# Transposes in an encoder trunk: squares of 32 on VectorE and a DRAM write and read in place of TensorE transposes

## The chip, the cores and the metric

The kernel runs on one core of a Trainium2 chip. The metric is the device time of one launch in microseconds (us). The engines are named as the profile names them: PE is the matrix engine (TensorE), PEld its weight loads, DVE is VectorE, ACT is ScalarE, POOL is GpSimd, and SP is the engine whose queue issues the DMAs (SPq).

## The reference

The reference is an encoder trunk of two layers over 256 tokens of width 2048, in float32. In each layer the normalised input `h` goes through one combined projection, which gives queries, keys and values of three attention branches, a gate path for each branch, and three merge gates:

```python
for l in range(DEPTH):
    h = rmsnorm(x, pre_norm_g[l])
    proj = jnp.einsum('bsd,dn->bsn', h, w_in[l])
    (qa, ka, va, qb, kb, vb, qc, kc, vc, za, zb, zc, gates) = jnp.split(proj, split_points, axis=-1)
    ya = neighbourhood_attention(heads(qa, 8), heads(ka, 8), heads(va, 8), rpb[l])
    qb_h = axial_rope(rmsnorm(heads(qb, 8), q_norm_g[l]))
    kb_h = axial_rope(rmsnorm(heads(kb, 2), k_norm_g[l]))
    yb = gqa_attention(qb_h, kb_h, heads(vb, 2))
    yc = dilated_mixture(heads(qc, 12), heads(kc, 12), heads(vc, 12))
    ga, gb, gc = jnp.split(sigmoid(gates + b_gate[l]), 3, axis=-1)
    merged = (ga * ((ya * silu(za)) @ w_branch_a[l]) + gb * ((yb * silu(zb)) @ w_branch_b[l])
              + gc * ((yc * silu(zc)) @ w_branch_c[l]))
    x = x + rmsnorm(merged @ w_out[l], post_norm_g[l])
```

## The kernel before

The 256 tokens are two tiles T of 128. All weights are streamed from DRAM in chunks of 256 rows by 512 columns (512 KB): `emit_raw` (L155 to L166) loads a chunk on SP's queue, `emit_hi` (L171, ACT) rounds it to a high part `wh`, and `emit_lo` (L176, DVE) takes the rest `wl`. `run_half` (L192) multiplies a chunk for one token tile. Each product is made of three one-pass matmuls (`mm3`, L143 to L148: high by high, high by low, low by high), so one chunk is 12 matmuls of 512 columns. There are 704 chunks: 8 for each block of 512 output columns of the combined projection and of the output projection, 4 or 2 for each block of the branch products.

The order of the work is written out by hand. The loop at the end of `trunk` (L737 to L753) goes through the chunks; `ahead` (L179) issues loads up to 6 chunks ahead, high parts up to 3 ahead and low parts up to 2 ahead. After each chunk `slot` (L100) puts in side work: two steps of the block evacuations in `evq`, one step of each generator in `active`, and one new job, from the queue `light` if it has one that is due, else from `heavy`. A `yield` ends a job's step for that slot. Each engine and SP's queue work in this program order.

Most tiles (`U`, L59) come from one pool of 47 buffers of 4 KB a partition.

A projection arrives with tokens on the partitions; what is contracted next must have columns on the partitions. So there are transposes on PE, [128,128] by an identity, four side by side in a bank of PSUM `tp`:

- `tr_job` (L280, its matmuls L284) for queries, keys and gate paths: one job for each token tile, started in the slot after the evacuation (or one later). ACT and DVE then split `tp` into high and low (L130, L132), or ACT copies it (L289).
- `head_job` (L360), 16 heads a layer of branches A and B: scores, softmax and norm in two slots; two slots on, four transposes of the probabilities (L380) and one split; two slots on, the product with the values `o` and `gate`. Heads start two slots apart (the 2 in `heavy`).
- `job_c` (L407), 4 merged heads a layer: the same with four transposes for each tile (L140 by `four_T`), heads four slots apart.
- `mt_job` in `merge` (L568): four transposes for each tile of the merged branches (L140), split into `MT[nb]`, the stationary operand of the output projection. `merge(3)` is followed at once by `out_block(0)`, whose chunk 6 (of 0 to 7) is the first to use `MT[3]`.
- `ht_psum` (L247): the next layer's input, also by `four_T`.

All DMAs are issued by SP in program order: chunks, the gate biases (`bg`, L553), the post-norm gains (L605), `x` (L73, L600).

Of the kernel before, what the change touches and what calls it, by code (L numbers as in the profile page):

```python
# [20 lines left out]
P = 128  # L21
GRID_W = 64
EPS = 1e-6
# [8 lines left out]
class Blk:  # L32
    """One 512-column block of a projection: K chunks of 256 rows, both token tiles."""
# [14 lines left out]
def trunk(ctx, tc, x, xT, wpack, wbr_a, wbr_b, wbr_c, wout, pre_g, qk_g, bgate, post_g, abias,  # L48
# [32 lines left out]
    # the engines wake while the first loads are under way  # L81
# [8 lines left out]
    evq, light, heavy, active = deque(), deque(), deque(), []  # L90
    flow = dict(cool=0, hold=True, slot=0, split=9)

    def later(g, wait=0):
        """a filler for a following slot, once what it needs is under way"""
        light.append((flow["slot"] + wait, g))
# [26 lines left out]
    def rsqrt(v, n):  # L122
        """1/sqrt of a small positive f32 tile"""
        y = small.tile([P, n], F32, name="rs_y")
        nc.gpsimd.tensor_tensor(out=y, in0=v, in1=mhalf[:, :n], op=ALU.pow)
        return y

    def split(src, h, lo, scale=1.0):
        """src * scale -> h + lo, both exactly representable for the one-pass products."""
# [6 lines left out]
    def four_T(src):  # L136
        """Four [128,128] transposes side by side in one bank."""
        tp = aux.tile([P, 4, P], F32, name="tp", bufs=2)
        for j in range(4):
            nc.tensor.transpose(tp[:, j, :], src(j), ident)  # L140
        return tp

    def mm3(out_, lhs, rhs, first, last):  # L143
        """out_ += lhs.T @ rhs for (high, low) pairs: one-pass products"""
# [60 lines left out]
    prev = {}  # L205

    def layer(l):
# [6 lines left out]
        # -- the layer's input: hT = (x * gain) transposed, 1/rms kept apart --  # L214
# [24 lines left out]
        def ht_x(nb, js):  # L239
            """from the host's transposed layout of x"""  # L240
# [6 lines left out]
        def ht_psum(nb, T):  # L247
            """from the previous layer's output: residual, transposes"""
# [30 lines left out]
        # -- evacuations, per token tile --  # L279
        def tr_job(dst, tok, T, n=4):  # L280
            """token-major [tok, n x 128] -> dst[column, block, tokens of T]; a pair is split"""
            tp = aux.tile([P, 4, P], F32, name="tp", bufs=2)
            for j in range(n):
                nc.tensor.transpose(tp[:, j, :], tok[:, T, j * P:(j + 1) * P], ident)  # L284
            c = slice(T * P, (T + 1) * P)
            if isinstance(dst, tuple):
                split(tp[:, 0:n], dst[0][:, 0:n, c], dst[1][:, 0:n, c])
            else:
                nc.scalar.copy(dst[:, 0:n, c], tp[:, 0:n])  # L289
            yield  # L290

        def evac_qk(store, key, which, two):
            tok = {}

            def f(T, ps):
# [4 lines left out]
                later(tr_job(store[key], tok[0], T))  # L300
# [16 lines left out]
        def evac_z(key):  # L317
            tok = {}

            def f(T, ps):  # L320
# [6 lines left out]
                later(tr_job(SZ[key], tok[0], T), 1)  # L327
# [3 lines left out]
        # -- attention --  # L331
        def softmax(sc, p, n, w, f=None):
            """n x w logits a row: exp(f * (s - max)), and the sums"""
# [11 lines left out]
        def norm(p, sm, n, rsh):  # L345
            """rows divided by their sums, times the gate's factor of the token"""
# [13 lines left out]
        def head_job(zb, hh, q, k, v, bias=None, f=None):  # L360
            """one head over all 256 keys, both token tiles: q, k give (high, low) of [d, tokens],
            v those of [keys of a tile, d]"""
# [14 lines left out]
            tp = aux.tile([P, 2, 256], F32, name="tp", bufs=2)  # L377
            for T in range(2):
                for kk in range(2):
                    nc.tensor.transpose(tp[:, kk, T * P:(T + 1) * P], p[:, T, kk * P:(kk + 1) * P], ident)  # L380
            pp = U("pp", [2, 2, 256], FR)
            ph, pl = pp[:, 0], pp[:, 1]
            split(tp, ph, pl)
# [23 lines left out]
        def job_c(hh, dist):  # L407
            """one merged head: the three groups' keys under one softmax"""
# [24 lines left out]
            px = U("px", [2, 256])  # L433
            for T in range(2):
                c = slice(T * P, (T + 1) * P)
                tp = four_T(lambda j: ps_[T][:, 0, j * P:(j + 1) * P])
                split(tp[:, 0:2], ph[:, :, c], pl[:, :, c])
                nc.scalar.copy(px[:, :, c], tp[:, 2:4])
                yield
# [10 lines left out]
        # -- branch A: two units of four heads --  # L450
# [17 lines left out]
        # -- branch B --  # L468
# [10 lines left out]
        def rope(dst, ps, T, n, which):  # L479
            """dst = rotation of ps (n heads), the norm's gain in the tables; in two steps"""  # L480
# [15 lines left out]
        def head_norm(ps, T, n):  # L496
            """1/rms of each head (of the normalised input's projection)"""
# [8 lines left out]
        def evac_qb(u):  # L506
            tok = {}

            def f(T, ps):
# [7 lines left out]
                later(tr_job(QT["b", u], tok[0], T), 1)  # L517
                if T == 1:
                    for hh in range(4):
                        heavy.append((2, job_b(u, hh)))  # L520
            return f

        def evac_kvb(T, ps):
# [14 lines left out]
            later(tr_job(KT["b"], tok, T, n=2), 1)  # L538
# [7 lines left out]
        # -- gates and branch products --  # L546
        def merge(nb):
# [20 lines left out]
            def mt_job(T):  # L568
                if nb not in MT:
                    MT[nb] = pair("mT", [4, 256])  # L570
                h, lo = MT[nb]
                c = slice(T * P, (T + 1) * P)
                tp = four_T(lambda j: G[0][:, T, j * P:(j + 1) * P])
                split(tp, h[:, :, c], lo[:, :, c], scale=0.5)
                yield

            def evac_p(i):
                def f(T, ps):
# [3 lines left out]
                    if i == 1:  # L582
                        later(mt_job(T))
# [268 lines left out]
```

## Time and profile before

| what | value |
|---|---|
| median of 3 runs | 2075.62 us (2074.99 to 2075.86) |
| span of the profiled execution, first to last instruction | 2073.5 us |
| median less that span (what lies around it) | 2.1 us |
| PE busy | 2061.9 us (99%), 9634 matmuls |
| DVE busy | 1163.2 us (56%) |
| ACT busy | 951.4 us (46%) |
| moved by DMA | 397.81 MB, mean 192 GB/s |
| TensorE clock granted | 9 in every slice (90% of full speed or more), mean 0.999 |

The profile is of one execution. Its own time outside the profiler is not given apart from its span, so the span and the 2.1 us that the median lies above it stand for it. Busy shares are of the span. A row such as `L284 PE MATMUL tp<-ident,tok` names the line, the engine, the operation, and the tile written from the tiles read. PE's durations overlap, because matmuls are pipelined; what one costs is read from the distance between starts.

### The profile page before, as it was taken

How to read it: one execution, taken by the hardware profiler on the slowest of the kernel's cores; microseconds unless marked ns; L12 is line 12 of the kernel's file. 1: busy time of each engine (PE TensorE's matmuls, PEld its weight loads, DVE VectorE, ACT ScalarE, POOL GpSimd, SP SyncE). 2: the span in 40 equal slices, each digit the busy share in tenths (PEclk: the TensorE clock that was granted, in tenths of full speed). 3: DMA queues.
4: the chain of work that ended last, by engine and by line, in shares of the span. 5: the costliest groups of instructions: out<-in, count | busy, mean ns of one | idle time of the engine just before them, and what ended most of it. 6: DMA issues, size and time to landing. Idle time of an engine off the chain costs nothing.

```text
span 2073.5 us, 24944 instructions
## 1 busy us (share of the span) xinstructions
PE 2061.9 (99%) x9634; PEld 1716.2 (83%) x9634; DVE 1163.2 (56%) x1445; ACT 951.4 (46%) x1370; POOL 23.2 (1%) x31
## 2 busy tenths in 40 slices
PE   9999999999999999999999999999999999999998
PEld 7888888888888888888888888888888888888886
DVE  6444466565776554645554445565657764646454
ACT  6443354444554434443564444454445543443332
POOL 0000000000000000000000000000000000000000
PEclk9999999999999999999999999999999999999999
DMA  9555455645546655667565554555454466656662
GB/s 373 190 173 187 153 173 179 213 156 185 168 163 208 203 198 188 203 228 259 174 228 171 188 183 142 182 176 200 164 187 163 168 213 200 197 191 208 228 241 71
DMA packets 115270, 397.81 MB, mean 192 GB/s; under 512 B 12752, under 2 KB 12880, under 8 KB 115152
## 3 DMA queue, kind: packets, MB, share of 16 engines
q1 hardware_dynamic: 115152, 396.23, 56.5%
q8 instruction: 75, 1.23, 0.2%
q14 instruction: 43, 0.35, 0.1%
HBM read 391.99 MB, written 4.19 MB: 191 GB/s over the span
## 4 chain that ended last, share of the span: by engine, by line
PE 99%; DMA 0%; ACT 0%; DVE 0%; SPq 0%; issue 0%; DVEq 0%; POOLq 0%; ACTq 0%
PE acc L148 31%; PE acc L146 31%; PE acc L147 31%; PE tp L284 1%; PE tp L140 1%; PE tp L380 1%; PE o L148 0%; PE sc L148 0%; PE o L147 0%; PE sc L147 0%; PE o L146 0%; PE sc L146 0%; DMA raw<-in_wpack_dram 0%; PE o L446 0%; PE sc L418 0%; DVE x L597 0%
## 5 line engine op out<-in xcount | busy, mean ns | idle before, releaser
L176 DVE TENSOR_TENSOR wl<-raw,wh 128x1024 fp32r<-128x1024 f32 (+1 forms) x706 | 831.7, 1217 | 172.1 <-ACT wh L171 169.3
L146 PE MATMUL acc<-wh,hTh 128*128 128x512 f32 x2240 | 886.3, 396 | 0.6 <-ACT wh L171 0.6
L147 PE MATMUL acc<-wl,hTh 128*128 128x512 f32 x2240 | 873.8, 390 | 0.8 <-DVE wl L176 0.8
L148 PE MATMUL acc<-wh,hTl 128*128 128x512 f32 x2240 | 873.8, 390 | 0.0
L171 ACT CAST wh<-raw 128x1024 fp32r<-128x1024 f32 (+1 forms) x706 | 699.3, 1043 | 40.0 <-DVE wl L176 12.9
L148 PEld LDWEIGHTS acc<-wh,hTl 128*128 128x128 f32 x2240 | 420.6, 188 | 89.0
L147 PEld LDWEIGHTS acc<-wl,hTh 128*128 128x128 f32 x2240 | 421.5, 188 | 84.9 <-DVE wl L176 2.6
L146 PEld LDWEIGHTS acc<-wh,hTh 128*128 128x128 f32 x2240 | 421.2, 188 | 83.3 <-ACT wh L171 1.6
L564 ACT ACTIVATE g<-g 128x512 f32<-128x512 f32 x48 | 30.4, 633 | 232.8 <-DVE g L563 232.8
L563 DVE SCALAR_TENSOR_TENSOR g<-acc,rsx,bg 128x512 f32<-128x512 f32 x48 | 35.9, 747 | 173.6 <-PE acc L148 173.6
L146 PE MATMUL acc<-wh,yTh 128*128 128x512 f32 x320 | 124.5, 389 | 0.0
L147 PE MATMUL acc<-wl,yTh 128*128 128x512 f32 x320 | 124.5, 389 | 0.0
L148 PE MATMUL acc<-wh,yTl 128*128 128x512 f32 x320 | 124.5, 389 | 0.0
L146 PE MATMUL acc<-wh,mTh 128*128 128x512 f32 x256 | 100.4, 392 | 0.0
L148 PE MATMUL acc<-wh,mTl 128*128 128x512 f32 x256 | 99.7, 390 | 0.0
L147 PE MATMUL acc<-wl,mTh 128*128 128x512 f32 x256 | 99.7, 389 | 0.0
L299 ACT ACTIVATE tok<-acc,rsx 128x512 f32<-128x512 f32 x40 | 27.6, 689 | 124.9 <-PE acc L148 124.9
L340 ACT ACTIVATE sp<-sp,nm 128x256 f32<-128x256 f32 (+1 forms) x48 | 27.6, 577 | 109.4 <-DVE nm L335 109.4
L579 DVE SCALAR_TENSOR_TENSOR g<-g,acc 128x512 f32<-128x512 f32 x48 | 32.8, 683 | 78.6 <-PE acc L148 78.6
L147 PEld LDWEIGHTS acc<-wl,yTh 128*128 128x128 f32 x320 | 60.1, 188 | 12.5
L146 PEld LDWEIGHTS acc<-wh,yTh 128*128 128x128 f32 x320 | 60.1, 188 | 12.5
L130 ACT ACTIVATE mTh<-tp 128x512 fp32r<-128x512 f32 x16 | 9.6, 598 | 132.4 <-PE tp L140 132.4
(116 smaller groups left out, 1172.2 us busy)
## 6 DMA issues: line engine op xcount, KB each, us to landing
raw<-in_wpack_dram SPq DMA_DIRECT2D x558, 512.0 KB, 3.5
raw<-in_wo_dram SPq DMA_DIRECT2D x64, 512.0 KB, 5.2
raw<-in_wa_dram SPq DMA_DIRECT2D x32, 512.0 KB, 3.3
raw<-in_wb_dram SPq DMA_DIRECT2D x32, 512.0 KB, 3.7
raw<-in_wc_dram SPq DMA_DIRECT2D x16, 512.0 KB, 3.8
bg<-in_bgate_dram SPq DMA_DIRECT2D x24, 256.0 KB, 3.8
x<-in_x_dram SPq DMA_DIRECT2D x8, 512.0 KB, 7.9
abias<-in_abias_dram SPq DMA_DIRECT2D x8, 512.0 KB, 4.2
```

The lines of the kernel that those rows point to most:

```text
L140: nc.tensor.transpose(tp[:, j, :], src(j), ident)
L146: nc.tensor.matmul(out_, lhsT=lh, rhs=rh, start=first, stop=False)
L147: nc.tensor.matmul(out_, lhsT=lh, rhs=rl, start=False, stop=False)
L148: nc.tensor.matmul(out_, lhsT=ll, rhs=rh, start=False, stop=last)
L171: nc.scalar.copy(HI[i][:, k], RAW[i][:, k])
L176: nc.vector.tensor_tensor(out=LO[i][:, k], in0=RAW[i][:, k], in1=f32(HI[i][:, k]), op=ALU.subtract)
L284: nc.tensor.transpose(tp[:, j, :], tok[:, T, j * P:(j + 1) * P], ident)
L299: nc.scalar.activation(tok[0][:, T], ps, AF.Copy, scale=S[which][T])
L340: nc.scalar.activation(p[:, i], sc[:, i], AF.Exp, bias=nm[:, i:i + 1], scale=1.0 if f is None else f[:, i:i + 1], accum_out=sm[:, i:i + 1])
L563: nc.vector.scalar_tensor_tensor(g, ps, S["rs"][T], BG[i], op0=ALU.mult, op1=ALU.add)
L564: nc.scalar.activation(g, g, AF.Tanh, scale=0.5)
L579: nc.vector.scalar_tensor_tensor(G[i][:, T], G[i][:, T], 1.0, ps, op0=ALU.add, op1=ALU.mult)
```

## The change

`tr_job` handles both token tiles at once, and it, `head_job`, `job_c` and `mt_job` transpose by a new generator `turn`. For each token tile one DVE transpose works in squares of 32 by 32, reading every fourth element of a row into `tt`. One DMA on SP writes `tt` (512 KB with four blocks, 256 KB with two) to a DRAM tensor of its own, and two slots later one DMA on SP reads it back into `tx` with rows regrouped (pieces of 1 KB, or 512 B). Two slots after that the split or copy follows, from `tx` in SBUF, now in all cases one for each token tile. Between the split and the product `o` lie two slots, as before in `head_job`, one more than before in `job_c`. The merged branches are no longer halved in their split (`scale=0.5` falls away); the post norm makes up for it with 4 EPS in place of EPS at L619. The heads of branch B are put into `heavy` once their queries are split. `ht_psum` keeps PE's transposes.

```diff
+    def turn(srcs, n, tx):
+        tt = U("tt", [4, 2, n * 32])
+        for T in range(2):
+            nc.vector.transpose(out=tt[:, :, T].rearrange("p j (h a) -> p h j a", h=n),
+                                in_=srcs[T].rearrange("p (h b j) -> p h j b", h=n, j=4))
+        run = 2 * n * 32
+        flow["turn"] += 1
+        d = nc.dram_tensor(f"turn{flow['turn']}", (4 * P, run), F32, kind="Internal").ap()
+        nc.sync.dma_start(out=d.rearrange("(p j) r -> p j r", j=4), in_=tt.rearrange("p j t r -> p j (t r)"))
+        yield
+        yield
+        tx.append(U("tx", [4, 2, n * 32]))
+        nc.sync.dma_start(out=tx[0].rearrange("p i t r -> p i (t r)"), in_=d.rearrange("(i p) r -> p i r", i=4))
+        yield
+        yield
+    def turned(tx, T, n):
+        return tx[:, :, T].rearrange("p i (h a) -> p h i a", h=n)
+    def squares(t, T):
+        return t[:, :, T * P:(T + 1) * P].rearrange("p h (i a) -> p h i a", i=4)
...
-        def tr_job(dst, tok, T, n=4):
-            tp = aux.tile([P, 4, P], F32, name="tp", bufs=2)
-            for j in range(n):
-                nc.tensor.transpose(tp[:, j, :], tok[:, T, j * P:(j + 1) * P], ident)
-            c = slice(T * P, (T + 1) * P)
-            if isinstance(dst, tuple):
-                split(tp[:, 0:n], dst[0][:, 0:n, c], dst[1][:, 0:n, c])
-            else:
-                nc.scalar.copy(dst[:, 0:n, c], tp[:, 0:n])
-            yield
+        def tr_job(dst, tok, n=4, then=None):
+            tx = []
+            yield from turn([tok[:, T] for T in range(2)], n, tx)
+            for T in range(2):
+                src = turned(tx[0], T, n)
+                v = lambda t: squares(t[:, 0:n], T)
+                if isinstance(dst, tuple):
+                    split(src, v(dst[0]), v(dst[1]))
+                else:
+                    nc.scalar.copy(v(dst), src)
+            if then:
+                then()
...
-                later(tr_job(store[key], tok[0], T))
+                if T == 1:
+                    later(tr_job(store[key], tok[0]))
...
-            tp = aux.tile([P, 2, 256], F32, name="tp", bufs=2)
-            for T in range(2):
-                for kk in range(2):
-                    nc.tensor.transpose(tp[:, kk, T * P:(T + 1) * P], p[:, T, kk * P:(kk + 1) * P], ident)
+            tx = []
+            yield from turn([p[:, T] for T in range(2)], 2, tx)
             pp = U("pp", [2, 2, 256], FR)
             ph, pl = pp[:, 0], pp[:, 1]
-            split(tp, ph, pl)
+            for T in range(2):
+                split(turned(tx[0], T, 2), squares(ph, T), squares(pl, T))
...
+            tx = []
+            yield from turn([ps_[T][:, 0] for T in range(2)], 4, tx)
             for T in range(2):
-                c = slice(T * P, (T + 1) * P)
-                tp = four_T(lambda j: ps_[T][:, 0, j * P:(j + 1) * P])
-                split(tp[:, 0:2], ph[:, :, c], pl[:, :, c])
-                nc.scalar.copy(px[:, :, c], tp[:, 2:4])
-                yield
+                src = turned(tx[0], T, 4)
+                split(src[:, 0:2], squares(ph, T), squares(pl, T))
+                nc.scalar.copy(squares(px, T), src[:, 2:4])
+            yield
+            yield
...
-                later(tr_job(QT["b", u], tok[0], T), 1)
                 if T == 1:
-                    for hh in range(4):
-                        heavy.append((2, job_b(u, hh)))
+                    later(tr_job(QT["b", u], tok[0],
+                                 then=lambda: heavy.extend((2, job_b(u, hh)) for hh in range(4))), 1)
...
-            def mt_job(T):
-                if nb not in MT:
-                    MT[nb] = pair("mT", [4, 256])
-                h, lo = MT[nb]
-                c = slice(T * P, (T + 1) * P)
-                tp = four_T(lambda j: G[0][:, T, j * P:(j + 1) * P])
-                split(tp, h[:, :, c], lo[:, :, c], scale=0.5)
-                yield
+            def mt_job():
+                MT[nb] = pair("mT", [4, 256])
+                return tr_job(MT[nb], G[0])
...
-                    if i == 1:
-                        later(mt_job(T))
+                    if i == 1 and T == 1:
+                        later(mt_job())
...
-                    nc.vector.tensor_scalar(v, v, 1.0 / DM, EPS, op0=ALU.mult, op1=ALU.add)
+                    nc.vector.tensor_scalar(v, v, 1.0 / DM, 4 * EPS, op0=ALU.mult, op1=ALU.add)
```

## Rows read from the trace of the kernel before

**Rows 1.** The page: busy time of each engine, and what the chain that ended last holds.

```profile
PE 2061.9 (99%) x9634; PEld 1716.2 (83%) x9634; DVE 1163.2 (56%) x1445; ACT 951.4 (46%) x1370; POOL 23.2 (1%) x31
...
PE acc L148 31%; PE acc L146 31%; PE acc L147 31%; PE tp L284 1%; PE tp L140 1%; PE tp L380 1%; PE o L148 0%; PE sc L148 0%; PE o L147 0%; PE sc L147 0%; PE o L146 0%; PE sc L146 0%; DMA raw<-in_wpack_dram 0%; PE o L446 0%; PE sc L418 0%; DVE x L597 0%
```

**Rows 2.** Waits of the whole span: engine, line, awaited: us, times, longest.

```profile
ACT wh L171 <- DMA raw<-in_wpack_dram: 7.6, 7, 1.8
...
PEld acc L147 <- DVE wl L176: 2.6, 5, 0.9
```

**Rows 3.** Groups by line: PE's transposes (busy us, mean ns, idle before).

```profile
L284 PE MATMUL tp<-ident,tok 128*128 128x128 f32 x280 | 42.2, 272 | 0.0
L380 PE MATMUL tp<-ident,sp 128*128 128x128 f32 x128 | 19.1, 272 | 0.0
...
L140 PE MATMUL tp<-ident,sp 128*128 128x128 f32 x64 | 9.6, 272 | 0.0
...
L140 PE MATMUL tp<-ident,g 128*128 128x128 f32 x64 | 9.6, 272 | 0.0
```

**Rows 4.** Timeline of PE around one set of four transposes: start, us, instruction.

```profile
51.98 0.39 PE L148 MATMUL acc<-wh,hTl 128*128 128x512 f32 x1
52.21 0.60 PE L284 MATMUL tp<-ident,tok 128*128 128x128 f32 x4
...
52.88 0.39 PE L147 MATMUL acc<-wl,hTh 128*128 128x512 f32 x1
53.12 0.40 PE L148 MATMUL acc<-wh,hTl 128*128 128x512 f32 x1
```

**Rows 5.** Groups by line, shapes kept apart: the rows that price DVE's work.

```profile
L176 DVE TENSOR_TENSOR wl<-raw,wh 128x1024 fp32r<-128x1024 f32 x702 | 829.1, 1220 | 171.6 <-ACT wh L171 168.9 <-DMA raw<-in_wpack_dram 2.6
...
L581 DVE TENSOR_TENSOR g<-g 128x512 f32<-128x512 f32 x32 | 22.1, 692 | 1.1
...
L132 DVE TENSOR_TENSOR pp<-tp,pp 128x512 fp32r<-128x512 f32 x32 | 22.0, 688 | 21.1 <-ACT pp L130 21.1
...
L475 POOL TENSOR_TENSOR ropeg<-rope_c,gq 128x256 f32<-128x256 f32 x8 | 8.4, 1087 | 841.5 <-DMA gq<-in_qk_g_dram 841.5
...
L132 DVE TENSOR_TENSOR pp<-tp,pp 128x256 fp32r<-128x256 f32 x16 | 6.8, 424 | 22.1 <-ACT pp L130 22.1
```

**Rows 6.** Busy time of each engine in three stretches of layer 0.

```profile
340.00:380.00 40.00, 40.00 (x209) 34.16 (x208) 28.36 (x47) 19.93 (x37) 0.00 (x0) 1.00 0.51 166
440.00:480.00 40.00, 40.00 (x212) 34.24 (x211) 27.47 (x45) 19.94 (x36) 4.05 (x4) 1.00 0.51 173
520.00:640.00 120.00, 120.00 (x601) 101.46 (x600) 85.71 (x144) 64.94 (x126) 4.03 (x4) 1.00 0.52 173
```

**Rows 7.** DMA issues: count, KB each, median us from issue to landing.

```profile
raw<-in_wpack_dram SPq DMA_DIRECT2D x558, 512.0 KB, 3.5
raw<-in_wo_dram SPq DMA_DIRECT2D x64, 512.0 KB, 5.2
...
x<-in_x_dram SPq DMA_DIRECT2D x8, 512.0 KB, 7.9
...
x_dram<-x SPq DMA_DIRECT2D x8, 256.0 KB, 3.0
...
gq<-in_qk_g_dram SPq DMA_DIRECT2D x2, 256.0 KB, 3.9
```

**Rows 8.** Timeline of SP and of ACT around the first gate block of layer 0.

```profile
523.93 0.42 SPq L553 DMA_DIRECT2D bg<-in_bgate_dram  x1
...
559.10 0.28 ACT L501 ACTIVATE junk<-acc 128x128 f32<-128x128 f32 x1
```

**Rows 9.** Timeline of PE, DVE and SP where the output projection of layer 0 begins.

```profile
946.28 0.39 PE L146 MATMUL acc<-wh,mTh 128*128 128x512 f32 x1
...
948.30 0.69 DVE L581 TENSOR_TENSOR g<-g 128x512 f32<-128x512 f32 x1
...
952.16 0.38 SPq L73 DMA_DIRECT2D x<-in_x_dram  x1
```

More of the change, by code (lines that the diff above doesn't have):

```diff
@@ L90, in trunk @@
     evq, light, heavy, active = deque(), deque(), deque(), []
-    flow = dict(cool=0, hold=True, slot=0, split=9)
+    flow = dict(turn=0, cool=0, hold=True, slot=0, split=9)
     def later(g, wait=0):
@@ L326, in f @@
                 nc.vector.scalar_tensor_tensor(z, z, 1.0, ps, op0=ALU.add, op1=ALU.mult)
-                later(tr_job(SZ[key], tok[0], T), 1)
+                if T == 1:
+                    later(tr_job(SZ[key], tok[0]), 1)
                 yield
@@ L537, in evac_kvb @@
                 nc.scalar.activation(t, t, AF.Copy, scale=f[:, i:i + 1])
-            later(tr_job(KT["b"], tok, T, n=2), 1)
+            if T == 1:
+                later(tr_job(KT["b"], tok, n=2), 1)
         def go_c():
```

## The prediction

> **What bounds the kernel now.** I read the page first: PE is busy 99% of the span and DVE 56%, and by line the chain that ended last is nearly all PE: the three lines of the products with 31% each, and lines L284, L140 and L380, the transposes, with about 1% each [rows 1]. So PE's instruction stream is the time, and the transposes stand in it. Next the waits: over the whole span PE's weight loads waited 2.6 us for a low part, and ACT waited 7.6 us for a chunk's load [rows 2]. Everything that feeds PE is early. A change pays here if it takes instructions from PE and leaves the feeders early.
>
> **What leaves PE.** The groups by line count the transposes that go: 280 for projections (L284), 128 for the heads of A and B (L380), 64 for the merged heads and 64 for the merged branches (both L140) [rows 3]. That is 536: 132 sets of four and, for the keys of branch B, 4 sets of two. Their mean of 272 ns is not their price, since they overlap. The price is in the timeline of PE [rows 4]. Two neighbouring products start 0.23 us apart (51.98 to 52.21). From the start of the set at 52.21 to the third start after it (53.12) are 0.91 us, in which also two products started: 0.91 - 2 x 0.23 = 0.45 us a set. 132 x 0.45 + 4 x 0.23 = 60.3 us. No engine stood idle for them on PE's side (idle before them 0.0 [rows 3]), so all of it is on the path.
>
> **What comes in.** There are 42 turns a layer, 84 in all: 25 a layer with four blocks (10 for queries and keys of A and C, 5 gate paths, 2 queries of B, 4 merged heads, 4 merged branches) and 17 with two (16 heads, keys of B).
>
> *DVE.* Each turn has two transposes, of 512 or of 256 elements a partition. The trace shows no transpose on DVE. From below, the nearest rows are ordinary operations of these sizes: 0.69 us for 512 from SBUF, 0.42 us for 256 [rows 5]. A gain is excluded: the split that DVE did before stays. From above I take the slowest engine's rate per element: POOL's 1087 ns for 256 [rows 5], so 2.17 us for 512. I take the lower row, since it is DVE's own; then DVE gets 50 x 2 x 0.69 + 34 x 2 x 0.42 = 98 us. The 32 heads of A and B split in two halves: 2 x 0.42 - 0.69 = 0.15 us each, 5 us. DVE goes from 1163 to 1266 us, 63% of the new span. What decides is its busiest stretch: 520 to 640 us, 85.7 of 120 us [rows 6]. Eight heads (0.99 each), the keys of B and two queries put 7.9 + 0.8 + 2.8 = 11.5 us there, while PE's part shrinks by 13 sets at most, 5.9 us: 97 of 114 us. That is 85%, still not a bound, so DVE's work costs nothing; its cover is PE. At the upper price it would be 85.7 + 18.6 + 2.2 + 8.7 = 115 of 114, no cover at all.
>
> The stride speaks against the lower row: each square is read with every fourth float, 16 bytes apart, and no row shows that. The Trainium skill (SBUF — State Buffer, Door 1: The DMA port swizzle) says that SBUF is read in lines of 16 bytes and that each access which crosses to a new line pays; here every read would. It names no size, and no run here shows one; by it DVE's sum would lie above 98 us, and the second rival below is where that leads.
>
> *ACT* keeps its copies and high parts, in two halves for the 32 heads; at 46% busy [rows 1] PE hides that.
>
> *SP and the DMAs.* Each turn adds a write and a read to SP's queue. The nearest rows: 3.0 us to land for a 256 KB write (`x_dram<-x`), 3.5 for a 512 KB chunk, 3.9 for a 256 KB read in pieces of 512 B (`gq`) [rows 7]. Traffic grows by 50 x 1 + 34 x 0.5 = 67 MB on 398. In the busiest stretch it was 173 GB/s at a DMA share of 0.52 [rows 6]; 6.5 MB more in 114 us make 239 GB/s and a share near 0.72. There is room. POOL's queue gets nothing.
>
> The write waits for DVE's transposes, and two slots later the read waits for the write's landing. Behind both stand chunk loads on SP. How early these are is seen in the first gate block: its bias and first chunk were issued at 523.9, while the last evacuation of the block before it began on ACT at 559.1 [rows 8]. The loads run some 35 us ahead. The new waits pull SP back to where DVE works, since it cannot pass a write whose data isn't there; 6 chunks ahead in program order remain, 6 x 12 x 0.23 = 16.6 us, less 3.5 for landing and about 3 for a write that SP waits for. About 10 us are left. So the loads cost nothing; without that cover each turn would cost the write's 3 us.
>
> *Who waits for the turned data.* After a write come two slots (5.5 us at two chunks of 12 x 0.23), the read, two more, the split, and for heads two more before PE needs `pp`. Against 11.0 us up to the split stand 0.8 to 1.4 for the transposes, 3.0 and 3.9: 8.3 at most. A wait there would first hold ACT and DVE, which are 2 to 3 chunks ahead. Queries, keys and gate paths are needed a block later or more.
>
> One place is tight. The output projection starts right behind the last branch product, at 946.3, and its chunk 6 needs `MT[3]`, at 946.3 + 6 x 2.76 = 962.9 us. On DVE the last sum (L581) ends at 949.0 [rows 9]; then come one low part, 1.2 [rows 5], and two transposes, 1.4: 951.6. The write lands at about 955. Before the read SP issues a bias and 512 KB of `x` (before the change at 952.2 [rows 9]) and two chunks. Loads take 5.2 us here (`wo` [rows 7]), so the read lands at 960.2, and the splits (ACT 0.6, then twice 0.7 on DVE) end at 962.2. If the read queues behind those loads it is some 2 to 3 us later. I put 1.5 us of stall there, 3 us in two layers.
>
> **Sum.** Against the profiled execution: 2073.5 - 60.3 + 3 = 2016.2 us of span, and with the 2.1 us by which the median lies above it 2018.3, so **2018**.
>
> **Rivals.**
>
> *DVE's transposes are slow.* For it: the stride above, and the busy stretches. Against it: no row of DVE is so slow. At 2.17 us for 512 the stretch of 520 to 640 would be over by 1 us. The heads of A at 340 to 380 (28.4 of 40) and at 440 to 480 (27.5) each get four heads (4 x 2.3) and a turn of four blocks (4.3): 42 and 41 us against 37, over by 5 and 4. Ten a layer, 20 in all: 2038.
>
> *SP is held by the turns, and the kernel gets slower.* Place: the heads of A and B, one each two slots, so one write and one read on SP in each 5.5 us. If SP's hold (about 1.7 us until DVE has split and turned, plus the write's landing) is longer than that, chunks arrive more slowly than PE eats them. At a landing of 7.9, the row of `x` in the crowded start [rows 7], the hold is 9.6, 4.1 too long, for 32 heads 131 us: 2149. It decides the sign from 60 / 32 = 1.9 us too long, a landing of 5.7. Against it: DMA shares of 0.51 to 0.52 in these stretches [rows 6], where a 256 KB write should land in 3.
>
> *The gain doesn't come.* PE would idle where the transposes stood, as another engine sets the pace: 2076. Against it: the idle times in front of the transposes are 0.0 [rows 3], and feeders are waited for some 10 us in all [rows 2].
>
> **How the numbers follow.** The forecast gets 0.76, slow transposes 0.14, the held queue 0.07, no gain 0.03. About 0.2%, or 4 us, can be told from no change. Forecast and first rival are both faster: 0.90; same 0.03; slower 0.07. The range must hold 8 in 10. Its low end is the sum without the stall (2015.3), less 3 for sets priced from starts rounded to 0.01 us. The high end takes in the first rival with a stall of 3 us at each of the two ends of merging as well, 2044: **2012 to 2044**.
>
> **What would show it.** Right: no rows of `tp` but those of `ht_psum` (32); PE's chain still over 97%; a span near 2016; DVE near 1266 us, with transposes near 0.69 and 0.42 us; new waits of SP for DVE and for writes, without PE behind them. The tight place would be a wait of PE for `mT` once a layer. Slow transposes would be rows over 1 us, and PE waiting for `wl`. A held queue would be ACT waiting for `raw` far more than 7.6 us. I am wrong if PE's idle time grows by more than 10 us, or if a set of transposes gave back clearly less than 0.45 us.

## The result, and the profile of the changed kernel

The changed kernel takes **2045.5 us** (median of 4 runs, 2041.5 to 2046.4) against 2075.3 for the kernel before beside it: ratio 0.9853, with an interval of 0.9839 to 0.9867. It is 1.5% faster. The gain is 30 us where I forecast 57, and the time lies 1.5 us above the high end of the range.

The page of the changed kernel, busy time and the chain that ended last (against [rows 1]):

```profile
PE 2014.1 (99%) x9098; PEld 1666.8 (82%) x9098; DVE 1294.6 (63%) x1645; ACT 959.0 (47%) x1402; POOL 24.0 (1%) x31
...
PE 89%; DVE 5%; ACT 2%; DMA 2%; issue 1%; SPq 0%; DVEq 0%; ACTq 0%; POOLq 0%
PE acc L171 29%; PE acc L172 29%; PE acc L170 29%; DMA tx<-turn 2%; DVE wl L200 1%; DVE tt L148 1%; ACT wh L195 1%; DVE nm L364 0%; ACT sp L369 0%; DVE pp L132 0%; PE sc L172 0%; PE sc L446 0%; DVE sp L380 0%; PE o L172 0%; PE o L171 0%
```

The first line could pass for a success: PE is still 99% busy. But 1% is 20 us here: PE is not busy for 2043.2 - 2014.1 = 29 us, against 11.6 before. The chain tells more: PE holds 89% of it and DVE 5%, where PE alone made nearly all of it before.

Waits of the changed kernel over the whole span, first of ACT and PE, then of SP's queue (us, times, longest; against [rows 2]):

```profile
ACT wh L195 <- DMA raw<-in_wpack_dram: 217.8, 49, 14.9
...
PEld acc L171 <- DVE wl L200: 12.7, 15, 2.4
...
PE acc L171 <- DVE wl L200: 7.4, 11, 2.0
...
PE acc L170 <- ACT mTh L130: 3.8, 2, 2.0
...
PE sc L172 <- DVE qkl L132: 3.7, 2, 1.8
```

```profile
SPq L153 <- DVE tt L148: 640.2, 59, 21.3
...
SPq L157 <- DMA turn<-tt: 82.6, 71, 4.5
```

SP now stands 640 us in front of the write, waiting for DVE's transposes, and then issues the chunk loads that stand behind it in a burst. ACT's wait for chunks grew from 7.6 to 217.8 us. Those two are the largest new waits, and run e12 below shows that they need cost PE nothing. The short waits of PE are what costs.

DVE's transposes, shapes kept apart (busy us, mean ns; the price that [rows 5] could only bound), and the DMAs of the turns and of two kinds of chunk (count, KB, median us to landing; against [rows 7]):

```profile
L148 DVE STREAM_TRANSPOSE tt<-tok 128x512 f32<-128x512 f32 x68 | 71.2, 1086 | 0.0
L148 DVE STREAM_TRANSPOSE tt<-sp 128x256 f32<-128x256 f32 x64 | 37.2, 620 | 0.0
```

```profile
raw<-in_wpack_dram SPq DMA_DIRECT2D x558, 512.0 KB, 6.5
raw<-in_wo_dram SPq DMA_DIRECT2D x64, 512.0 KB, 9.2
turn<-tt SPq DMA_DIRECT2D x50, 512.0 KB, 3.0
tx<-turn SPq DMA_DIRECT2D x50, 512.0 KB, 5.5
...
turn<-tt SPq DMA_DIRECT2D x34, 256.0 KB, 2.2
tx<-turn SPq DMA_DIRECT2D x34, 256.0 KB, 4.3
```

**Where PE stands idle.** I went along PE's timeline and took from each distance between two starts the undisturbed one (0.227 us for 512 columns, 0.12 for 256 and 0.11 for 128, the distances in stretches where PE waits for nothing). The sum of what is over is 10.6 us in the kernel before and 40.3 us in the changed one: 29.7 us of new lost time. Without it the span of 2043.2 us would be 2013.5. After the start of the kernel, 22 distances are over by more than 0.25 us and make 22.1 us (before: 4, making 1.4), and 45 are over by about 0.2 us and make 8.9 us (before: none).

PE's timeline at three of these places of layer 0 (start us, us, instruction, idle before it and what ended it): the first scores of branch B, the chunk products among B's heads, and the output projection's first use of `MT[3]`.

```profile
535.78 0.39 PE L170 MATMUL sc<-kb,qkh 128*128 128x256 f32 x1 [0.90 <-ACT qkh L130]
...
538.11 0.39 PE L172 MATMUL sc<-kb,qkl 128*128 128x256 f32 x1 [1.83 <-DVE qkl L132]
...
607.13 0.50 PE L171 MATMUL acc<-wl,hTh 128*128 128x512 f32 x1 [2.02 <-DVE wl L200]
...
608.62 0.63 PE L171 MATMUL acc<-wl,hTh 128*128 128x512 f32 x1
609.05 0.63 PE L172 MATMUL acc<-wh,hTl 128*128 128x512 f32 x1
609.48 0.63 PE L170 MATMUL acc<-wh,hTh 128*128 128x512 f32 x1
...
944.86 0.50 PE L170 MATMUL acc<-wh,mTh 128*128 128x512 f32 x1 [1.96 <-ACT mTh L130]
```

The same places come back in layer 1. The lines at 608.62 to 609.48 are the 0.2 us kind: shortly after the idle of 2.02 us, matmuls start 0.43 us apart instead of 0.23. They are called slow starts below.

Added up by place, both layers together and slow starts included, lost us on PE in the profiled executions; the runs from e0 on are the experiments below:

| run | first scores of B | heads of B | `MT[3]` | heads of C | all else | sum |
|---|---|---|---|---|---|---|
| before | 0.0 | 0.7 | 0.1 | 0.6 | 9.2 | 10.6 |
| changed | 8.7 | 13.8 | 8.2 | 3.1 | 6.5 | 40.3 |
| e0 floor | 9.7 | 0.5 | 0.0 | 0.3 | 6.5 | 17.0 |
| e1 late | 0.0 | 10.1 | 5.3 | 2.8 | 9.1 | 27.3 |
| e2 `MT[3]` on PE | 9.9 | 13.9 | 0.1 | 2.7 | 7.8 | 34.4 |
| e3 no stride | 8.2 | 3.9 | 3.8 | 0.6 | 7.7 | 24.2 |
| e7 (e1 and e2) | 0.0 | 13.3 | 0.1 | 3.2 | 8.9 | 25.5 |
| e4 four reads | 0.0 | 4.6 | 0.1 | 5.1 | 17.2 | 27.0 |
| e8 e7, no stride | 0.0 | 4.5 | 0.0 | 0.9 | 7.7 | 13.1 |
| e9 e7, norm on ACT | 0.0 | 0.9 | 0.0 | 4.3 | 7.7 | 12.9 |
| e10 e7, more slots | 0.0 | 11.0 | 0.0 | 0.4 | 7.3 | 18.7 |
| e12 e9 and e10 | 0.0 | 0.5 | 0.0 | 0.3 | 6.9 | 7.7 |

### The profile page after: what moved, and what is told of

Read it like the earlier page. It is cut to its first block, busy times and chain, and to the rows that moved or that the text cites. A ratio compares the mean times of both kernels' runs of the same rounds, so it can differ in the third digit from the quotient of the medians.

```text
span 2043.2 us, 24560 instructions
## 1 busy us (share of the span) xinstructions
PE 2014.1 (99%) x9098; PEld 1666.8 (82%) x9098; DVE 1294.6 (63%) x1645; ACT 959.0 (47%) x1402; POOL 24.0 (1%) x31
## 4 chain that ended last, share of the span: by engine, by line
PE 89%; DVE 5%; ACT 2%; DMA 2%; issue 1%; SPq 0%; DVEq 0%; ACTq 0%; POOLq 0%
PE acc L171 29%; PE acc L172 29%; PE acc L170 29%; DMA tx<-turn 2%; DVE wl L200 1%; DVE tt L148 1%; ACT wh L195 1%; DVE nm L364 0%; ACT sp L369 0%; DVE pp L132 0%; PE sc L172 0%; PE sc L446 0%; DVE sp L380 0%; PE o L172 0%; PE o L171 0%
## 5 line engine op out<-in xcount | busy, mean ns | idle before, releaser
L170 PE MATMUL acc<-wh,hTh 128*128 128x512 f32 x2240 | 877.4, 392 | 0.4 <-ACT wh L195 0.4
L195 ACT CAST wh<-raw 128x1024 fp32r<-128x1024 f32 (+1 forms) x706 | 703.4, 1043 | 346.9 <-DMA raw<-in_wpack_dram 217.8
L148 DVE STREAM_TRANSPOSE tt<-tok 128x512 f32<-128x512 f32 (+1 forms) x72 | 73.5, 1060 | 0.0
L172 PEld LDWEIGHTS acc<-wh,yTl 128*128 128x128 f32 x320 | 60.1, 188 | 12.4
```

Source lines behind the costliest of these rows:

```text
L148: nc.vector.transpose(out=tt[:, :, T].rearrange("p j (h a) -> p h j a", h=n), in_=srcs[T].rearrange("p (h b j) -> p h j b", h=n, j=4))
L170: nc.tensor.matmul(out_, lhsT=lh, rhs=rh, start=first, stop=False)
L172: nc.tensor.matmul(out_, lhsT=ll, rhs=rh, start=False, stop=last)
L195: nc.scalar.copy(HI[i][:, k], RAW[i][:, k])
```

## The experiments

All are edits of the changed kernel, and each ran beside the kernel before. My theory was that the 60.3 us did leave PE and that new stalls in three places took half of it back. The rivals were that a set of transposes gives back less than 0.45 us, and that the held loads or late reads are the cost.

**e0_floor: the turns taken out, their slots kept.**

```diff
     def turn(srcs, n, tx):
-        (two transposes, the write, the read)
         yield
         yield
+        tx.append(srcs)
         yield
         yield
```

> Leaves out the transposes themselves: no DVE squares, no DRAM write and read; the splits read the untransposed source, and every job keeps its slots. So only PE's shorter stream is left of the change. Theory 1 (the 60.3 us that leave PE are real, and all that was lost afterwards are new stalls of PE): 2013 to 2016 us. Rival (the sets gave back clearly less than 0.45 us each): above 2025 us.

Measured: 2021.9 us, ratio 0.9745 (0.973 to 0.9759), some 6 us over the expectation and below the 2025 of the rival. What is lost on PE is 17.0 us, and what is new lies at one place, B's first scores and the slow starts behind them (9.7 us), with the same two idle times as above (0.9 and 1.8 us in each layer). So that stall needs no transpose and no DMA. It comes from the order: the heads of B enter `heavy` in the slot that issues the split of their queries, so their scores stand on PE right behind a split that ACT and DVE have still to do.

**e1_late: B's heads enter two slots later.**

```diff
             if then:
+                yield
+                yield
                 then()
```

> The heads of branch B are put into heavy two slots after the split of their queries instead of in the same slot. Theory 1 (in each layer PE stands at the first scores of B, because they are issued in the slot of the split that they need; 3.5 and 5.1 us by PE's starts): 8 us less than the changed kernel, about 2037 us, with no PE wait for qkh or qkl left. Rival (DVE's load in the stage of B is the limit, and the heads only shift): same as the changed kernel, 2045 us.

Measured: 2032.7 us, ratio 0.9799 (0.9783 to 0.9816), 12.8 us below the changed kernel, where 8 were expected. The waits of PE for `qkh` and `qkl` are gone (8.7 us by the table), and the heads of B and `MT[3]` lose 3.7 and 2.9 us less in this execution. Those 6.6 us are mostly slow starts: the changed kernel's trace has 37 of its 45 at these two places, e1's has 3 in all, although the idle times there are about as long as before. So some 4 of the 12.8 us are not shown to come from the edit.

**e5_floor_late: both edits.** This is the test of the 60.3 us.

> Leaves out the transposes as the floor run does, and puts the heads of B two slots after the split of their queries. If the 7 us by which the floor lay above 2015 are the stall at the first scores of B, and nothing else: 2014 to 2016 us. If the sets gave back less than 0.45 us each: 2019 us or more.

Measured: 2013.3 us, ratio 0.9701 (0.9685 to 0.9717). It lies 0.7 us under the expected range, and 62 us under the kernel before. The PE part of the sum stands, and the rival that a set gives back less falls.

**e2_mt_pe: only the last merged branch transposes on PE**, two sets in each layer.

```diff
+                if nb == 3:
+                    return mt_pe()
                 return tr_job(MT[nb], G[0])
+            def mt_pe():
+                h, lo = MT[nb]
+                for T in range(2):
+                    c = slice(T * P, (T + 1) * P)
+                    tp = four_T(lambda j: G[0][:, T, j * P:(j + 1) * P])
+                    split(tp, h[:, :, c], lo[:, :, c])
+                    yield
```

> Only the last block of merged branches of each layer, MT[3], goes back to PE's transposes. Theory 1 (the read of MT[3] queues behind x and chunks and is late for chunk 6; 4.2 and 4.0 us by PE's starts): those 8.2 us less 4 sets of 0.45 us, 6.4 us less than the changed kernel: about 2039 us. Rival (chunks held back on SP are what is late there): the stall moves to PE waiting for wh or wl, time within 2 us of the changed kernel.

Measured: 2039.4 us, ratio 0.9828 (0.9813 to 0.9842): 6.1 us less, as the theory had it. With the 4 x 0.45 = 1.8 us that PE pays for the four sets, the stall was worth 7.9 us in two layers, where I had put 3.

**e3_dense: the transposes read their source without the stride.**

```diff
-                                in_=srcs[T].rearrange("p (h b j) -> p h j b", h=n, j=4))
+                                in_=srcs[T].rearrange("p (h j b) -> p h j b", h=n, j=4))
```

> The DVE transposes read neighbouring elements instead of every fourth; everything else, the DMAs too, stays, so the transposed data come out with their columns in another order. Theory A (the 16-byte stride is what makes a transpose of 512 take 1.07 us and one of 256 take 0.62): 0.69 and 0.42 us, DVE 50 us less busy, and about 8 to 12 us less time, from the stage of the heads of B. Rival B (a transpose costs that much in itself): 1.07 and 0.62 us again, and 2045 us.

Measured: 2031.1 us, ratio 0.9787 (0.9772 to 0.9801). DVE's transposes, shapes kept apart:

```profile
L148 DVE STREAM_TRANSPOSE tt<-tok 128x512 f32<-128x512 f32 x68 | 44.1, 687 | 0.0
L148 DVE STREAM_TRANSPOSE tt<-sp 128x256 f32<-128x256 f32 x64 | 24.4, 420 | 0.0
```

Without the stride they take 687 and 420 ns, the values that I had taken from ordinary operations; with it 1086 and 620. The stride alone costs 0.4 us on 512 and 0.2 us on 256 elements. DVE's busy time falls by 51 us and the kernel by 14.4, somewhat over the 8 to 12 expected: most of DVE's work is hidden, and somewhere it is not. By the table that is among the heads of B (13.8 to 3.9 us) and at `MT[3]` (8.2 to 3.8), slow starts included.

**e7_late_mt: e1 and e2 together.**

> Heads of B two slots late and MT[3] by PE, squares still with the stride. If the stalls are separate: 2045.5 - 12.8 - 6.1 = 2027 us, and what is left over the floor is DVE in the stage of the heads of B. Rival (each takes away part of the same stall): 2031 us or more.

Measured: 2031.1 us, ratio 0.9784 (0.9769 to 0.9799). The two gains of 12.8 and 6.1 do not add, and by its number the run lies where the rival put it. By place it doesn't: the stalls at the scores and at `MT[3]` are both gone, and the heads of B lose 13.3 us, as in the changed kernel, and not the 10.1 of e1. Nearly all of that difference is slow starts. The same idle of PE, 2.0 us near 610, is followed by seven of them in e7 and by none in e1, and it is alike in layer 1 (eight and none). Why they follow one such idle and not the other stays open.

**e4_late_mt_dense4: e7, and the stride moved into the DMAs**: the write orders rows so that the columns come out in their places in spite of the dense transposes, and the read becomes four reads of 32 partitions.

> All three together, with the right result: heads of B two slots late, MT[3] by PE, and DVE squares that read neighbouring elements; to put the columns in their places the DRAM tensor is written by one DMA with rows in another order and read by four DMAs of 32 partitions each. Theory (three separate stalls, which add up: 12.8, 6.1 and 14.4 us in the single runs): the floor without transposes and without the stall at B, about 2015, plus 4 sets of 0.45 us and some rest: 2016 to 2020 us. Rival (four reads where there was one hold SP longer and land later): above 2025 us, with ACT waiting for tx.

Measured: 2035.4 us, ratio 0.9806 (0.9791 to 0.982). The gain on DVE shows among B's heads (4.6 us lost in place of 13.3) and is lost again elsewhere. From the issue of the first of the four reads to the landing of the last are 6.1 us (median), against 4.9 for the one read of e7, and 11.1 at most. PE has new stalls of 2.1 and 2.8 us for `wl` at 402 and 1414, where ACT had waited 4.2 us for a read before it could round the next chunk.

**What is left in e7.** Four runs were made for it. The theory: among the heads of B, where a head follows each second chunk, DVE sets the pace. PE needs 24 x 0.227 + 12 x 0.12 = 6.9 us for two chunks and a head; DVE starts the softmax of successive heads 7.25 us apart (8.45 where the work of a block's evacuation comes between).

**e8_late_mt_dense: e7 with the dense transposes of e3.**

> e7's two edits, and the transposes read their source without a stride (columns come out permuted; the output is not the reference's). Theory: what is left in e7 is DVE as the bound among the heads of B. There e7's heads follow each other 7.25 us apart, DVE busy 35.1 of 42 us, while PE's own work for two chunks and a head is 24 x 0.227 + 12 x 0.12 = 6.9; with transposes of 0.42 in place of 0.62 a head costs DVE 0.4 less, so 6.85 and no stall: e7's 12.8 us of idle around 600 and 1610 go, 2031 - 13 = 2018 (2016 to 2021), distances of 6.9, DVE's transposes 0.69 and 0.42. Rival (the stall there comes from the turn's wait on the read, not from DVE's pace): 2028 to 2031, distances near 7.2.

**e9_act_norm: e7 with the norm's multiplications of B's heads on ACT.**

```diff
-                nc.vector.tensor_scalar(p[:, i], p[:, i], r[:, i:i + 1], None, op0=ALU.mult)
+                if act:
+                    nc.scalar.activation(p[:, i], p[:, i], AF.Copy, scale=r[:, i:i + 1])
+                else:
+                    nc.vector.tensor_scalar(p[:, i], p[:, i], r[:, i:i + 1], None, op0=ALU.mult)
...
-            norm(p, sm, 2, S["rsh2"])
+            norm(p, sm, 2, S["rsh2"], act=f is not None)
```

> e7's two edits, and in the heads of B the two multiplications of the norm (0.31 us each on DVE) go to ACT, which is busy 23 of 42 us there. The transposes stay at 0.62. Theory (DVE's pace is the bound among the heads of B): 0.6 us a head less on DVE, distances 6.9 in place of 7.25, the 12.8 us of e7 go down to 3 or less: 2018 to 2022. Rival (the hop to ACT and back puts ACT's queue into DVE's: DVE waits for ACT behind high parts of 1.04 us): 0.5 to 1 us of wait a head, 2030 or more.

**e10_more_slots: e7 with one more slot between read and split**, for turns of four blocks (the line in `tr_job` gives it to the keys of B too).

```diff
             yield from turn([tok[:, T] for T in range(2)], n, tx)
+            yield
...
             yield from turn([ps_[T][:, 0] for T in range(2)], 4, tx)
+            yield
```

> e7's two edits, and one more slot between the read and the split of every turn of four blocks (projections, merged branches, heads of C). Theory (DVE's pace among the heads of B decides what is left): these turns stall PE 2.5 us in all (heads of C near 300 and 1310), so 2028 to 2031. Rival (reads that land in the bursts of loads hold ACT, and that is most of what is left): 2022 or less, and ACT's waits for reads gone.

**e11_b_heads_pe: e7 with the transposes of B's heads on PE**, as before the change.

> e7's two edits, and the 16 heads of B (8 a layer) transpose on PE as before the change, without write, read and their four slots. Theory: PE pays 16 x 0.45 = 7.2 us for them, and the 12.8 us of idle go: 2031 - 12.8 + 7.2 = 2025.5 (2023 to 2028). Rival (the idle there has another cause than the turns of these heads): 2031 + 7 = 2038.

Measured: e8 2019.5 us (ratio 0.9731, 0.9717 to 0.9746), e9 2019.7 (0.9729, 0.9713 to 0.9745), e10 2026.1 (0.9763, 0.9748 to 0.9777), e11 2026.2 (0.9761, 0.9746 to 0.9775). All three ways of taking work from DVE among B's heads brought what the theory said. The heads' stretch in e7, e8, e9 and e11, one fence each (stretch; its length, then busy us and count of PE, PEld, DVE, ACT, POOL; granted clock, DMA share, GB/s):

```profile
570.00:612.00 42.00, 38.62 (x187) 31.68 (x186) 35.09 (x73) 23.15 (x48) 0.00 (x0) 0.97 0.62 214
```

```profile
570.00:612.00 42.00, 40.39 (x206) 34.17 (x205) 34.81 (x74) 24.02 (x49) 0.00 (x0) 1.00 0.68 234
```

```profile
570.00:612.00 42.00, 42.00 (x214) 35.76 (x214) 35.05 (x65) 28.41 (x59) 0.00 (x0) 1.00 0.71 242
```

```profile
570.00:612.00 42.00, 42.00 (x228) 36.29 (x227) 31.57 (x60) 22.69 (x42) 0.00 (x0) 1.00 0.48 157
```

DVE's busy share is 84% in e7 and 83% in e9, which hardly differ; but e7's PE did 187 matmuls in this time and e9's 214. The share does not tell who is the bound, and neither does DVE's sum alone. One turn of the loop in e7, from one head's softmax to the next, and in it the two waits of ACT and DVE for each other:

```profile
577.61:584.85 7.24, 7.24 (x41) 6.26 (x40) 6.03 (x15) 3.71 (x8) 0.00 (x0) 1.00 0.65 222
```

```profile
578.58 0.57 ACT L371 ACTIVATE sp<-sc,nm,bf 128x256 f32<-128x256 f32 x1 [3.56 <-DVE nm L368]
...
581.07 0.76 DVE L132 TENSOR_TENSOR pp<-tx,pp 128x256 fp32r<-128x256 f32 x2 [1.11 <-ACT pp L130]
```

DVE is busy 6.03 of the 7.24 us, less than the 6.9 that PE needs. The rest is mostly the 1.11 us in which it waits for ACT's part of a split; ACT has that split behind the exponentials, and these wait for DVE's maximum (`nm`). So the pace is that of DVE's order with this wait in it. Whether a shorter wait alone would do as well wasn't run. The pace follows what is taken from DVE: heads 7.25 us apart in e7, 6.85 in e8, 6.58 in e9, against the 6.9 that PE needs. The theory had 6.9 for e9; it came to 6.58, and DVE then catches up on PE. In e8 4.5 us are still lost there, where the theory had none. e10 leaves the pace at 7.25 and removes the stalls of the heads of C; its 5 us lie between theory and rival. Of the 6.8 us that its trace loses less, 2.8 are the heads of C, 2.3 the heads of B, which have 8 slow starts in place of 15, and 1.6 lie elsewhere.

**e12_act_norm_slots: e9 and e10 together.**

> e9's edits, and one more slot between the read and the split of the turns of four blocks, as in e10. Theory: e9's rest of idle is the heads of C (1.2 and 2.3 us at 300 and 1310), which the slot takes away, as it took them from e7: 2016 to 2018. Rival (e10's 5 us against e7 came from fewer drops of the clock in other places that e9 has no longer): 2019 to 2020, the same as e9.

Measured: **2015.0 us** (2014.5 to 2015.4), ratio 0.9708 (0.9694 to 0.9723), 1 us below what the theory said; the heads of C lose 0.3 us in place of 4.3. This version has every part of the computation and is the fastest of these: 60 us below the kernel before and 30 below the changed one. Its busy times and chain, and its waits of ACT and of PE's loads:

```profile
PE 2001.3 (99%) x9114; PEld 1663.3 (83%) x9114; DVE 1284.6 (64%) x1609; ACT 976.6 (49%) x1434; POOL 24.0 (1%) x31
...
PE 99%; DMA 0%; ACT 0%; DVE 0%; SPq 0%; issue 0%; DVEq 0%; POOLq 0%; ACTq 0%
```

```profile
ACT wh L195 <- DMA raw<-in_wpack_dram: 218.5, 79, 14.9
...
PEld acc L171 <- DVE wl L200: 2.4, 4, 0.9
```

ACT waits for chunks as long as in the changed kernel (218.5 us), and PE's lost time is 7.7 us, less than the 10.6 before the change. So the held queue and its bursts cost PE nothing once DVE keeps pace, splits find their reads landed, and the stalls at the scores and at `MT[3]` are taken away.

**e6_pool_queue: the turns' writes and reads on POOL's queue**, so that SP is never held.

```diff
-        nc.sync.dma_start(out=d.rearrange(
+        nc.gpsimd.dma_start(out=d.rearrange(
...
-        nc.sync.dma_start(out=tx[0].rearrange(
+        nc.gpsimd.dma_start(out=tx[0].rearrange(
```

> The changed kernel with the DMAs of the turns issued by POOL, so that SP's queue holds chunks, biases and x alone. Theory 1 (chunks held back on SP cost ACT its head start, not PE's time): ACT's 217 us of waits for raw fall under 50 us, MT[3] comes somewhat earlier, and the time stays within 5 us of the changed kernel, 2040 to 2046 us. Rival (SP's hold is what costs PE): below 2035 us.

Measured: 2129.6 us, ratio 1.0258 (1.0242 to 1.0273), slower than the kernel before. A miss, and no rival had it. ACT's waits for chunks did fall, to 7.8 us, as the theory had it: it is SP's hold that makes them. Waits of ACT in this run, and the turns' DMAs:

```profile
ACT mTh L130 <- DMA tx<-turn: 122.5, 7, 25.6
...
ACT qkh L130 <- DMA tx<-turn: 118.8, 14, 14.1
...
ACT pp L130 <- DMA tx<-turn: 91.7, 19, 10.3
```

```profile
turn<-tt POOLq DMA_DIRECT2D x50, 512.0 KB, 4.9
tx<-turn POOLq DMA_DIRECT2D x50, 512.0 KB, 6.1
```

By the medians over all turns, from the last transpose's end to the landed read are 0.30 + 4.4 + 0.60 + 5.5 = 10.8 us, against 0.03 + 2.9 + 0.06 + 5.0 = 8.0 on SP's queue. Add the transposes (1.2 to 2.2 us) and a turn no longer fits the 11.0 us of its four slots; ACT, which works in order, stands in front of the split, and the chunks' high parts wait behind it.

**e13_wide_sp and e14_wide_pool: e9 with three slots after the write and three after the read**, on SP's and on POOL's queue.

> e9's edits, and every turn gets three slots in place of two both after the write and after the read (16.5 us in place of 11.0 up to the split). Control for the next run. If reads that land late are all that is left: 2015 to 2018. If the longer life of the turn's buffers holds loads back: 2022 or more.

> The control with the turns' writes and reads on POOL's queue. In e6 a turn took 0.30 + 4.4 + 0.60 + 5.5 = 10.8 us from the last transpose to the landed read, against 2.9 + 0.1 + 5.0 = 8.0 on SP, and with 1 to 2 us for the transposes that is over the 11.0 us of its four slots. Theory (that is why e6 lost): with 16.5 us the loss goes, within 5 us of the control, and ACT's waits for reads fall from 460 us to under 100. Rival (POOL's queue costs by itself, by its instructions or its descriptors): 30 us or more over the control.

Measured: e13 2016.3 us (ratio 0.9716, 0.97 to 0.9732), as expected, and e14 2026.0 (0.9758, 0.9744 to 0.9773). With six slots in place of four, POOL's queue lies 10 us over its control, where e6 lay 84 over the changed kernel, and ACT's waits for the turns' reads fell from 461 to some 66 us. So most of e6's loss was the length of a turn against its slots, as far as these runs show it: e9's edits stand in both of them and not in e6. The 10 us are twice what the theory allowed: two stalls of 2.7 us among the heads of A (454 and 1461) and the slow starts behind them make most of it. Whether POOL's queue has a price of its own there stays open.

## Why the prediction was wrong

The sum held the 60.3 us and a stall of 3 us. The new lost time of PE was 29.7 us: 13.1 among the heads of B, 8.7 at B's first scores, 8.1 at `MT[3]` and 2.5 at the heads of C, with 2.7 less elsewhere. PE's idle time grew by more than 10 us, which the prediction had named as the sign of being wrong. Three steps failed: the work on DVE was put at nothing, one edit got no price, and the stall that it did have was too small.

**What leaves PE** was right. 60.3 us from the timeline [rows 3, 4]; e5, which has no transposes and no stall of its own, lies 62 us under the kernel before, and the changed kernel's span without its new lost time is 2013.5 against the 2013.2 of the sum without stalls.

**"97 of 114 us. That is 85%, still not a bound, so DVE's work costs nothing; its cover is PE."** This is the first and largest step that failed, in two ways. The price was too low: at 1.086 and 0.620 us the transposes cost DVE 100 x 1.08 + 68 x 0.62 = 150 us, where I took 98 (the upper price would have made 291). I chose the row that was DVE's own and of the same size, although the stride stood against it. The Trainium skill (SBUF — State Buffer, Door 1: The DMA port swizzle) has 16-byte lines and an access that pays when it crosses to a new one. I cited that and gave it only the 0.14 of a rival. Run e3 agrees with it in sign: 1.086 us with every fourth float, 0.687 without. And the average was the wrong view: the 120 us from 520 to 640 hold evacuations and heads, with different limits. Among the heads alone the time of one head decides, 7.25 us in DVE's order, the wait for ACT included, against 6.9 in PE's. 13.8 us of PE's time went there, about 4 of them slow starts. In e8, at the price that I took, it is 4.5 us.

**"The loads cost nothing"** was right, though the waits looked alarming. ACT's wait for chunks grew as the rival of the held queue wanted (217.8 us against 7.6), but ACT has high parts ready ahead of PE and stands that wait. e12 shows it: the same wait, and PE loses less than before the change.

**"I put 1.5 us of stall there, 3 us in two layers."** Right place, right mechanism, term too small: 7.9 us by e2. The write was issued at 932.25 and the read at 935.54, 3.3 us apart as I had it (951.6 and about 955), and the two transposes before them took 2.0 us, where I had put 1.4. But the read took 8.55 us to land, behind `bg`, `x` and two chunks, where I had put 5.2; the sentence "it is some 2 to 3 us later" was the better one. PE then stood 1.96 us, and about as much again went in the slow starts behind the idle. The write, the read, and ACT's start when the read had landed:

```profile
932.25 0.33 SPq L153 DMA_DIRECT2D turn<-tt  x1
...
935.54 0.66 SPq L157 DMA_DIRECT2D tx<-turn  x1
...
944.17 1.15 ACT L130 ACTIVATE mTh<-tx 128x512 fp32r<-128x512 f32 x2 [1.74 <-DMA tx<-turn]
```

**Missed altogether**: the edit of a few words that puts B's heads into `heavy` once their queries are split. I described it and gave it no price. Before, they were queued at the evacuation and their scores came later than the split; now the scores of the first head are issued in the slot of the split. It is 8.7 us on PE's timeline; in the time of e1 it is 12.8, of which some 4 are slow starts that e1 lacks at other places. "Queries, keys and gate paths are needed a block later or more" is true of all but these queries.

**Who waits for the turned data.** "8.3 at most" against 11.0 us was about right in the middle (1 to 2 us of transposes and 8.0 of DMAs, 9 to 10), and wrong at the ends: reads that land in a burst of loads took up to 8.6 us. With a slot more, the heads of C lose 2.8 us less in e10 than in e7, and 4.0 less in e12 than in e9.

**The rivals.** Slow transposes (the first of the three, which the prediction calls the second where it speaks of the stride) was half true: 1.09 and not 2.17 us, with a bound among the heads of B and not of A, and it stood too low at 0.14. The low price came from ordinary operations, and e3 measured just that without the stride, 0.687 and 0.420 us; so the choice of row was right for a dense transpose and the stride is what it left out. The held queue didn't happen, and neither did the gain that doesn't come.

## What to carry to other kernels

Before a busy share is called cover, cut the stretch down to the loop that repeats, and compare the time that one turn of it takes in each engine's order, with the waits in it that two engines have for each other: an engine that was busy 84% of the time was the bound here. Give a price to every edit that moves the moment at which a job enters a queue, however short it is, and ask what the consumer then finds in front of it. A long new wait (640 us on SP, 218 on ACT) is harmless where the engine behind it has a lead, and a few waits of 2 us on the engine that is the bound are not.

## What was not expected of the hardware

A stall of PE costs more than its idle time. In the changed kernel the granted clock is 1.00 in nearly all stretches of 20 us, but after the stall at 607, and in four others, it is lower (0.83 to 0.91). Two stretches of the heads of B in layer 0 (columns as above; against [rows 6]):

```profile
580.00:600.00 20.00, 19.43 (x100) 16.39 (x99) 17.57 (x38) 9.62 (x22) 0.00 (x0) 1.00 0.67 239
600.00:620.00 20.00, 17.04 (x73) 13.63 (x72) 14.86 (x25) 9.94 (x17) 0.00 (x0) 0.91 0.68 245
```

A mean of 0.91 is a stretch at 2.4 GHz with a part at 1.2: the rows from 608.62 on start 0.43 us apart, where 0.23 is usual. Behind five of the idles of about 2 us there are 8 to 12 such starts, 45 in all, 8.9 us or nearly a third of the new lost time; in the kernel before and in e12, which have no such idle, there are none. The stall at B's first scores brought eight in layer 1 and none in layer 0, and e1 has four idles of 1.9 to 2.6 us (excess over the usual start distance) with two slow starts behind them in all, so an idle of 2 us does not always do it. What decides it is not shown. The 3.2 us between e1 and e7 among the heads of B are nearly all such starts.

The stride's price on DVE's transpose (0.40 us on 128x512, 0.20 on 128x256) and the longer landing of a write on POOL's queue (4.9 us against 3.0 for 512 KB) are the other two.
